# Softmax of the global branch in one scaling pass, with two query blocks side by side and one transpose for their meta columns

## The chip, the cores and the metric

The kernel runs on one core of a Trainium2 chip. A core has five engines that work side by side: TensorE (PE in the profile, its weight loads PEld) for matrix products and transposes, VectorE (DVE), ScalarE (ACT), GpSimd (POOL), and SyncE (SP), which issues most DMAs here. The metric is the device time of one execution in microseconds; a kernel's time is the median of its runs. Work happens in SBUF (128 partitions) and in PSUM, eight banks of 128 x 512 floats, into which TensorE writes. All data are float32; a product takes its operands as two parts each, "hi" (rounded for TensorE) and "lo" (the rest), so that one product is three matmuls.

## What is computed

The reference is two layers of an encoder over 512 grid tokens (64 x 8) and 16 learned meta tokens, 528 in all. Each layer normalises the stream, makes one wide projection and runs two branches side by side, whose gated outputs are merged and added to the stream. The change is in the first, the global branch:

```
def attend(qb):                                   # 8 query heads share 2 key/value heads
    s = einsum('bqkgd,bskd->bkgqs', qb, k) * HEAD_DIM ** -0.5
    p = softmax(s, axis=-1)
    return einsum('bkgqs,bskd->bqkgd', p, v)
```

Queries come in blocks of 128, every one against all 528 keys; the 16 meta queries form a block of their own. The second branch is a windowed attention, in which each query sees a window of 8 x 16 grid neighbours and the meta keys.

## The kernel before

The dense work is a row of projections (`product`, L277): each takes 128 output columns, has eight weight tiles, and for every span of tokens does 24 matmuls (L286 to L288) into a bank of the pool `pp`, which has two. Weights come by DMA into `raw`, ScalarE casts them (L216), GpSimd subtracts (L217). The first layer computes all 528 tokens in two spans of 264 ("full"); the second needs only the 512 grid tokens for most projections and does one span of 512.

Attention is woven between the projections by a clock of the kernel's own: after each span, and in the second layer also in the middle of one, `tick` (L273) is called. Two lists (`Side`, L247) hold the units of the windowed and of the global branch; a unit starts every four ticks, and its steps fall due at ticks after its start as the tables at L35 to L42 say. Within one tick the windowed list comes first. The tile framework then puts each engine's instructions into one fixed order, mostly that of the program; what is traced under `high_priority` goes ahead, and `issue_after(ins)` keeps an instruction behind `ins` in its engine's queue.

A unit of the global branch (`global_unit`, L712) is one head and two blocks of 128 queries; there are 16 in each layer, and two units for meta queries in the first. Its steps:

- `softmax` (L697) for each block: four matmuls (L499, L500) write the scores of 128 queries against 528 keys into the tile `S`, two banks, of which there is only one (it serves the windowed branch's scores `Sb` too). VectorE takes the negated maximum (L704), multiplies it by the query's scale (L705, the per-query norm factor, or 0.125), ScalarE takes the exponential straight from PSUM with that scale and bias and sums it (L706), VectorE inverts the sum (L708) and multiplies (L709).
- `transposes` (L722): the 512 grid columns of both blocks, four 128 x 128 transposes to a bank of the pool `tp`, which has two; then `split` (L170) into hi and lo.
- `meta_transposes` (L734): the last 32 columns of each block, 16 grid and 16 meta keys, transposed one block at a time into the tile `ptm`, and split by `split_down` (L688) into the tile `ga`.
- `sums` (L742): nine matmuls (L746) with the values, and `unit_done` (L770), which puts the two halves of the result together (`combine`, L672) and, after a head pair, applies the gate.

Keys: after their projection `rotated` (L423) applies the rotary positions in a tile of tag E; the norm factors are spread by `pair_factors` (L562), two copies on VectorE ahead of the transposes at L601 and L604, and `keys_scaled` (L598) multiplies them in and calls `stack_soon` (L481), which makes the hi and lo key tiles of both key heads: three ScalarE copies, three VectorE subtractions, two DMAs. `scaled` (L630) and `values` (L636) do the values likewise; the meta tile of the values has rows 0 to 15 cleared. In the windowed branch, `sums` (L876) puts its result together at once (L887, L891).

Buffers in SBUF go by tag (L107); those with tag M hold the input, the stacked queries, the exponentials P and the gated results, 16 single tiles.

Of the kernel before, what the change touches and what calls it, by code (L numbers as in the profile page):

```python
# [18 lines left out]
P = 128  # L19
# [72 lines left out]
def trunk_kernel(ctx: ExitStack, tc: tile.TileContext, xT, w, gn, gf, bias, rope, out):  # L92
# [13 lines left out]

    BUFS = {"h": 16, "M": 16, "O": 8, "K": 4, "T": 2, "R": 2, "B": 9, "E": 6, "G": 8, "KB": 4, "KR": 2, "raw": 3, "whi": 4, "wlo": 4}  # L107

    def slot(tag, name, dt=F32):
        return slots.tile([P, NKEY if tag in ("KB", "KR") else NTOK], dt, tag=tag, bufs=BUFS[tag], name=name)  # L110

# [6 lines left out]

    zero = cpool.tile([P, P], F32, name="zero")
    nc.vector.memset(zero, 0.0)  # L120
# [150 lines left out]
    side_na, side_gqa = Side(NA_AT_TICK), Side(GQA_AT_TICK)  # L271

    def tick():  # L273
# [88 lines left out]
    def feature(k):  # L362
        xs.append(slot("M", f"x0_{k}"))
        nc.sync.dma_start(xs[k], xT[k])
        h.append(normed(0, k, xs[k], NTOK))
        done[0] = h_last["hi"].ins
# [35 lines left out]
    for l in range(DEPTH):  # L402
# [14 lines left out]
        def sum_squares(j, n, qh, ql):  # L417
            for i, (a, b) in enumerate(((0, HALF), (HALF, n))):
                for v in (qh, ql):
                    nc.tensor.matmul(mps[:10, i, :b - a], sel_h[j], v[:, a:b], start=j == 0 and v is qh,  # L420
                                     stop=j == 4 and v is ql, skip_group_check=True)

        def rotated(c, g, full, name):  # L423

            n, j = NTOK if full else NREAL, c - QA
            q, sq = slot("E", f"{name}{l}_{c}"), slot("G", f"{name}s{l}_{c}")
            qh, ql = slot("G", f"{name}h{l}_{c}", F32R), slot("G", f"{name}l{l}_{c}", F32R)
# [20 lines left out]

        def halves_of(tag, name, x, n, eng):

            hi = slot(tag, name, F32R)
# [8 lines left out]
        def stack_q(tag, name, q, n, eng):  # L460

            hi, lo = halves_of(tag, name + "b", q, n, eng)
            first = slot(tag, name + "a", F32R)
            move(first, up, hi, up, n)
            move(first, down, lo, up, n)
            move(hi, up, lo, down, n)
            return first, hi

        def stack_k(tag, name, k, n, eng):

            both = []
            for i, t in enumerate(halves_of(tag, name + "h0", k, n, eng)):
# [8 lines left out]
        def stack_soon(tag, name, k, n):  # L481

            pairs = []
            for hh, r in enumerate((up, down)):
                kh, kl = slot(tag, f"{name}h{hh}", F32R), slot(tag, f"{name}l{hh}", F32R)
# [76 lines left out]
        def pair_factors(t, c, n, name):  # L562

            f = slot("G", f"pf{name}{l}") if n > 1 else tiny.tile([P, P], F32, tag="pf", bufs=1, name=f"pf{name}{l}")
            f = f[:, :P * n].rearrange("p (n h d) -> p n h d", n=n, h=2)
            nc.vector.tensor_copy(f, st["r3"][:, t, c].rearrange("p t (n h) -> p (t n) h", h=2).unsqueeze(3)
                                  .to_broadcast([P, n, 2, HD]))
# [30 lines left out]
        def keys_scaled():  # L598
# [29 lines left out]


        def scaled(tag, c, name, full):  # L630
            t = slot(tag, name)
            for ps, a, b in project(c, full):
                evac["v"] = nc.vector.tensor_mul(t[:, a:b], ps, rbc[:, a:b])
            return t

        def values(v, out, tiles, name):  # L636
# [7 lines left out]
            split(out[:n, u:u + e, :, 0], out[:n, u:u + e, :, 1], src)  # L644
            if n == 32:
                for p in (slice(0, 16), slice(64, P)):
# [4 lines left out]
        v = scaled("E", VA, f"va{l}", True)  # L651
# [4 lines left out]
        side_gqa.later(NORM_AT[l]["values"][1], lambda v=v, VA2=VA2: values(v, VA2, [(4, NTOK - 32, 32)], f"am{l}"))  # L656

# [14 lines left out]
        def combine(tag, o, hh, av, c0, n):  # L672
# [3 lines left out]
            nc.scalar.copy(t[r, :n], av[q, :n])  # L676
            nc.vector.tensor_add(o[r, c0:c0 + n], av[r, :n], t[r, :n])

        def gated(tag, o, gate, name):
            hi, lo = slot(tag, name + "h", F32R), slot(tag, name + "l", F32R)  # L680
# [7 lines left out]
        def split_down(t, tp, rows, a, b):  # L688

            with tc.high_priority():  # L690
                nc.scalar.copy(t[:rows, a:b], tp)
                nc.vector.tensor_sub(t[rows:2 * rows, a:b], tp, t[:rows, a:b].bitcast(F32))


        zgate, oa, o_t, newest = {}, [None] * 4, {}, {}

        def softmax(q, qs, kv, n, scale, name):  # L697
# [4 lines left out]
            p = slot("M", f"P{name}")  # L702
            with tc.high_priority():
                newest["max"] = nc.vector.tensor_reduce(st[:n, 0:1], S[:n, :, :HALF], axis=AX.XY, op=ALU.max, negate=True)  # L704
                nc.vector.tensor_scalar_mul(st[:n, 1:2], st[:n, 0:1], scale)  # L705
                nc.scalar.activation(p[:n].rearrange("p (i k) -> p i k", i=2), S[:n, :, :HALF], AF.Exp,  # L706
                                     bias=st[:n, 1:2], scale=scale, accum_out=st[:n, 2:3])
            nc.vector.reciprocal(st[:n, 3:4], st[:n, 2:3])  # L708
            nc.vector.tensor_scalar_mul(p[:n], p[:n], st[:n, 3:4])  # L709
            return p  # L710

        def global_unit(kv, parts, n, name, done):  # L712

            width = n * len(parts)
            per = min(4, 512 // width)
            c = {"p": [], "t": []}

            def scores(i):
                q, qs, scale = parts[i]
                c["p"].append(softmax(q, qs, kv, n, scale, f"{name}_{i}"))  # L720

            def transposes(kt):  # L722
                tp = bank(ps_t, f"pt{name}_{kt}", "tp")
                for i in range(per):
                    for t, p in enumerate(c["p"]):
                        o = width * i + n * t
                        transposed(tp[:, o:o + n], p[:n, P * (kt + i):P * (kt + i + 1)], n)
                th, tl = slot("G", f"pth{name}_{kt}", F32R), slot("G", f"ptl{name}_{kt}", F32R)
# [49 lines left out]
        def start_meta(kv):  # L778
            for j in (2 * kv, 2 * kv + 1):
                if j not in o_t:  # L780
                    o_t[j] = slot("T", f"oa{l}_{j}")
            return global_unit(kv, [(Q2m[kv], slice(0, 64), 0.125)], 64, f"m{l}_{kv}", lambda av: meta_done(kv, av))

# [14 lines left out]
        def windowed_head(hd):  # L798
# [77 lines left out]
            def sums():  # L876
# [7 lines left out]
                for i, (u, t, c0, a, b) in enumerate(seq):  # L884
                    nc.tensor.matmul(av[:, a:b], rows2(VB2[:, u, hh]), t[:, c0:c0 + b - a], start=i == 0,  # L885
                                     stop=i == len(seq) - 1, skip_group_check=True)
                combine("B", o, hh, av, 0, NREAL)  # L887
                if full:
                    av = bank(ps_t, f"avbm{nm}", "tp")
                    nc.tensor.matmul(av[:, :NMETA], rows2(VB2[:, 0, hh]), c["mt"], start=True, stop=True)  # L890
                    combine("B", o, hh, av[:, :NMETA], NREAL, NMETA)  # L891
                if hh == 1:
                    ob[j] = gated("M", o, zb[j], f"ob{l}_{j}")

# [68 lines left out]
        for m in range(8 + LAG):  # L963
            if m < 8:
                gates[m] = merge_gate(GB, m)
            if m == LAG - 1:
                side_na.finish()
            if m >= LAG:
                mb.append(slot("B", f"mb{l}_{m - LAG}"))
# [3 lines left out]
        for m in range(8 + LAG):  # L973
# [9 lines left out]
            if m >= LAG:  # L983
                ma = slot("G", f"ma{l}_{m - LAG}")
                hi, lo = slot("M", f"mxh{l}_{m}", F32R), slot("M", f"mxl{l}_{m}", F32R)
                end = m == 7 + LAG
# [126 lines left out]
```

## Time and profile before

| | us |
|---|---|
| median of 3 runs | 878.3 (878.14 to 878.75) |
| the profiled execution | 877.75 |
| its span | 876.0 |
| busy TensorE / weight loads | 858.6 / 791.1 |
| busy VectorE / ScalarE / GpSimd | 556.8 / 462.3 / 364.0 |
| granted TensorE clock, mean | 0.997 |

The profile is one execution. Its span goes from the first to the last instruction of the program; the time of the execution has a little around it. A busy share is time in which at least one instruction of the engine ran; matmuls overlap, so TensorE's busy time does not show how fast they followed each other. In the views, L704 is line 704 of the kernel, `P<-S,st` names tiles (output, then inputs, without buffer numbers), and the arrow in "idle before, releaser" says whose end let the instruction start. A wait for several things is put down to the one that came last by the profile.

### The profile page before, as it was taken

What the parts mean: (1) busy time and instruction counts of PE and PEld (TensorE: products, weight loads), DVE (VectorE), ACT (ScalarE), POOL (GpSimd) and SP (SyncE); (2) the same over time, 40 slices, a digit from 0 to 9 for tenths busy, and PEclk for the clock granted to TensorE, in tenths of its full rate; (3) what the DMA queues carried; (4) which work ended last, traced back from release to release, by engine and by line L of the source; (5) the groups of instructions that cost most, each with busy time, mean ns of one, the idle gap of its engine ahead of it and who ended that gap; (6) DMA issues with size and microseconds to landing.
All of it is one profiled execution on the core that took longest, in us unless ns stands there. A gap on an engine that the chain in (4) does not pass through costs nothing.

```text
span 876.0 us, 16169 instructions
## 1 busy us (share of the span) xinstructions
PE 858.6 (98%) x5984; PEld 791.1 (90%) x5984; DVE 556.8 (64%) x1264; ACT 462.3 (53%) x1027; POOL 364.0 (42%) x298
## 2 busy tenths in 40 slices
PE   9999999999999999999999999999999999999996
PEld 8999999999999999999998989888888888888785
DVE  6985678676774674436447757688867746544632
ACT  8644666565764554334345446566656645443422
POOL 5564343343233333454764643334332233334640
PEclk9999999999999999999999999999999999999998
DMA  8364444334222221324655654234432222222602
GB/s 278 109 161 123 112 120 118 89 110 122 73 71 74 73 74 61 109 86 143 168 129 128 158 160 129 79 109 133 124 109 73 76 81 73 85 84 97 205 24 97
DMA packets 67232, 96.90 MB, mean 111 GB/s; under 512 B 23376, under 2 KB 23888, under 8 KB 67152
## 3 DMA queue, kind: packets, MB, share of 16 engines
q1 hardware_dynamic: 66432, 94.79, 37.6%
q8 instruction: 47, 0.77, 0.4%
q10 hardware_dynamic: 720, 1.06, 0.3%
q14 instruction: 33, 0.27, 0.1%
HBM read 76.72 MB, written 4.19 MB: 92 GB/s over the span
## 4 chain that ended last, share of the span: by engine, by line
PE 83%; DVE 8%; ACT 5%; issue 2%; DMA 2%; POOL 0%; SPq 0%; POOLq 0%; ACTq 0%; DVEq 0%
PE pp L286 17%; PE pp L288 17%; PE pp L287 17%; PE y L288 3%; PE y L286 3%; PE y L287 3%; PE av L746 3%; PE pt L116 3%; PE avb L885 2%; PE S L500 2%; PE pf L1046 2%; PE pf L1048 2%; PE S L499 2%; PE pf L1047 1%; DVE Pb L827 1%
## 5 line engine op out<-in xcount | busy, mean ns | idle before, releaser
L217 POOL TENSOR_TENSOR wlo<-raw,whi 128x512 fp32r<-128x512 f32 x214 | 286.7, 1344 | 431.0 <-ACT whi L216 385.2
L286 PE MATMUL pp<-hh,whi 128*128 128x264 f32 (+1 forms) x1056 | 334.8, 317 | 1.8 <-DVE qb L943 1.0
L288 PE MATMUL pp<-hh,wlo 128*128 128x264 f32 (+1 forms) x1056 | 329.3, 312 | 0.0
L287 PE MATMUL pp<-hl,whi 128*128 128x264 f32 (+1 forms) x1056 | 328.2, 311 | 0.0
L216 ACT CAST whi<-raw 128x512 fp32r<-128x512 f32 x214 | 131.2, 620 | 157.6 <-PE pp L287 61.9
L286 PEld LDWEIGHTS pp<-hh,whi 128*128 128x128 f32 x1056 | 198.6, 188 | 12.0 <-DVE qb L943 1.2
L288 PEld LDWEIGHTS pp<-hh,wlo 128*128 128x128 f32 x1056 | 198.9, 188 | 10.8
L287 PEld LDWEIGHTS pp<-hl,whi 128*128 128x128 f32 x1056 | 199.3, 189 | 9.0
L706 ACT ACTIVATE P<-S,st,r 128x528 f32<-128x528 f32 x64 | 50.6, 790 | 52.7 <-DVE st L705 45.3
L953 DVE TENSOR_TENSOR mg<-pp,rbc 128x264 f32<-128x264 f32 (+1 forms) x48 | 24.8, 517 | 45.3 <-PE pp L288 44.5
L704 DVE TENSOR_REDUCE st<-S 128x1 f32<-128x528 f32 x64 | 45.0, 703 | 13.0 <-PE S L500 12.2
L173 DVE TENSOR_TENSOR ptl<-pt,pth 128x512 fp32r<-128x512 f32 x64 | 43.9, 687 | 13.1 <-ACT pth L172 12.6
L172 ACT CAST pth<-pt 128x512 fp32r<-128x512 f32 x64 | 37.3, 584 | 10.3 <-PE pt L116 9.3
L116 PE MATMUL pt<-ident,P 128*128 128x128 f32 x256 | 39.7, 274 | 2.0 <-DVE st L705 1.0
L708 DVE RECIPROCAL st<-st 128x1 f32<-128x1 f32 x64 | 10.5, 164 | 45.5 <-ACT P L706 45.1
L823 ACT ACTIVATE Pb<-Pb,stb 128x208 f32<-128x208 f32 (+1 forms) x64 | 31.0, 485 | 12.5 <-DVE stb L821 12.4
L287 PE MATMUL pp<-mxl,whi 128*128 128x264 f32 x128 | 36.5, 285 | 0.0
L286 PE MATMUL pp<-mxh,whi 128*128 128x264 f32 x128 | 36.5, 285 | 0.0
L288 PE MATMUL pp<-mxh,wlo 128*128 128x264 f32 x128 | 36.4, 284 | 0.0
L709 DVE TENSOR_SCALAR P<-P,st 128x528 f32<-128x528 f32 x64 | 34.7, 542 | 2.2
L954 ACT ACTIVATE mg<-mg 128x264 f32<-128x264 f32 (+1 forms) x48 | 23.7, 493 | 23.0 <-DVE mg L953 22.8
L746 PE MATMUL av<-pth,VA 128*128 128x256 f32 x128 | 35.1, 296 | 0.0
(611 smaller groups left out, 1765.7 us busy)
## 6 DMA issues: line engine op xcount, KB each, us to landing
raw<-in_w_dram SPq DMA_DIRECT2D x214, 256.0 KB, 2.7
bias<-in_bias_dram SPq DMA_DIRECT2D x16, 480.0 KB, 4.0
rawl<-in_w_dram SPq DMA_DIRECT2D x16, 256.0 KB, 3.1
x<-in_xT_dram SPq DMA_DIRECT2D x8, 264.0 KB, 4.6
xr<-in_xT_dram SPq DMA_DIRECT2D x8, 264.0 KB, 3.9
x1d<-xt SPq DMA_DIRECT2D x32, 64.0 KB, 2.8
xf<-x1d SPq DMA_DIRECT2D x8, 256.0 KB, 4.9
KB_0l<-kb SPq DMA_DIRECT2D x8, 140.0 KB, 2.6
```

The source lines that it names most:

```text
L116: nc.tensor.transpose(ps, src, ident[:n, :n])
L172: split_at["hi"] = nc.scalar.copy(hi, src)
L173: split_at["any"] = nc.vector.tensor_sub(lo, src, hi.bitcast(F32))
L216: cast = nc.scalar.copy(hi, raw)
L217: sub = nc.gpsimd.tensor_sub(lo, raw, hi.bitcast(F32))
L286: nc.tensor.matmul(ps, wh, rh[:, a:b], start=i == 0, stop=False)
L287: nc.tensor.matmul(ps, wh, rl[:, a:b], start=False, stop=False)
L288: nc.tensor.matmul(ps, wl, rh[:, a:b], start=False, stop=i == n - 1)
L704: newest["max"] = nc.vector.tensor_reduce(st[:n, 0:1], S[:n, :, :HALF], axis=AX.XY, op=ALU.max, negate=True)
L706: nc.scalar.activation(p[:n].rearrange("p (i k) -> p i k", i=2), S[:n, :, :HALF], AF.Exp, bias=st[:n, 1:2], scale=scale, accum_out=st[:n, ...
L709: nc.vector.tensor_scalar_mul(p[:n], p[:n], st[:n, 3:4])
L746: nc.tensor.matmul(c["av"], rows2(c["t"][i][0]), c["t"][i][1], start=i == 0, stop=i == 8)
```

## The change

Six edits belong together.

- The scores are multiplied by the query's scale and their maximum is taken in one VectorE pass that writes them to SBUF; ScalarE negates the maximum and takes the exponential in place, from SBUF, with scale 1.
- The two blocks' P lie side by side in one tile of 2 x 528 columns. The first block has its meta keys last and the second first, so that the four meta stretches of 16 columns meet in the middle, and one transpose of 64 columns serves both. For this the keys get a copy of their 16 meta columns in front (528 + 16), and the block chooses its stretch of 528. The meta tile of the values is laid out to match (64 rows).
- Tag M holds 8 pairs in place of 16 tiles. Keys move to a buffer of tag KR, values to one of tag `bias`.
- The key head 1 half of `stack_soon` comes four ticks later, and the two factor copies go to ScalarE.
- In the windowed branch, putting the sums together is deferred to the end of the tick.
- The additions of `combine` are kept behind the newest maximum in VectorE's queue.

```
-    BUFS = {"h": 16, "M": 16, ...
+    BUFS = {"h": 16, "M": 8, ...
...
+    def two(tag, name, dt=F32):
+        if tag == "M":
+            t = slots.tile([P, 2, NTOK], dt, tag=tag, bufs=BUFS[tag], name=name)
+            return t[:, 0], t[:, 1]
+        return slot(tag, name + "a", dt), slot(tag, name + "b", dt)
...
+    eighth = cpool.tile([P, 1], F32, name="eighth")
+    nc.vector.memset(eighth, 0.125)
...
     def tick():
         side_na.tick()
         side_gqa.tick()
+        while ending:
+            ending.pop(0)()
...
-            nc.vector.tensor_copy(f, st["r3"][:, t, c].rearrange("p t (n h) -> p (t n) h", h=2).unsqueeze(3)
+            nc.scalar.copy(f, st["r3"][:, t, c].rearrange("p t (n h) -> p (t n) h", h=2).unsqueeze(3)
                                   .to_broadcast([P, n, 2, HD]))
...
-            KA2.extend(stack_soon("K", f"KA{l}", k, NTOK))
+            both_ends = keys[0]
+            nc.vector.tensor_copy(both_ends[:, :NMETA], k[:, NREAL:])
+            KA2.extend(stack_soon("K", f"KA{l}", both_ends, NTOK + NMETA, 0))
+            side_gqa.later(4, lambda: KA2.extend(stack_soon("K", f"KA{l}", both_ends, NTOK + NMETA, 1)))
...
-            nc.vector.tensor_add(o[r, c0:c0 + n], av[r, :n], t[r, :n])
+            with ExitStack() as held:
+                if "max" in newest:
+                    held.enter_context(tc.issue_after(newest["max"].ins))
+                nc.vector.tensor_add(o[r, c0:c0 + n], av[r, :n], t[r, :n])
...
+        def split_meta(parts):
+            with tc.high_priority():
+                for g, (to, tp) in enumerate(parts):
+                    nc.scalar.copy(to[32 * g:32 * g + 32], tp[32 * g:32 * g + 32])
+                for g, (to, tp) in enumerate(parts):
+                    nc.vector.tensor_sub(to[64 + 32 * g:96 + 32 * g], tp[32 * g:32 * g + 32], to[32 * g:32 * g + 32].bitcast(F32))
...
-                score(S[:n, i, :HALF], q, KA2[kv], qs, slice(HALF * i, HALF * (i + 1)))
+                score(S[:n, i, :HALF], q, KA2[kv], qs, slice(k0 + HALF * i, k0 + HALF * (i + 1)))
...
-                newest["max"] = nc.vector.tensor_reduce(st[:n, 0:1], S[:n, :, :HALF], axis=AX.XY, op=ALU.max, negate=True)
-                nc.vector.tensor_scalar_mul(st[:n, 1:2], st[:n, 0:1], scale)
-                nc.scalar.activation(p[:n].rearrange("p (i k) -> p i k", i=2), S[:n, :, :HALF], AF.Exp,
-                                     bias=st[:n, 1:2], scale=scale, accum_out=st[:n, 2:3])
+                newest["max"] = nc.vector.tensor_tensor_reduce(
+                    p[:n].rearrange("p (i k) -> p i k", i=2), S[:n, :, :HALF], scale[:n].unsqueeze(2).to_broadcast([n, 2, HALF]),
+                    1.0, -3e38, ALU.mult, ALU.max, st[:n, 0:1])
+                nc.scalar.mul(st[:n, 1:2], st[:n, 0:1], -1.0)
+                nc.scalar.activation(p[:n], p[:n], AF.Exp, bias=st[:n, 1:2], scale=1.0, accum_out=st[:n, 2:3])
...
+            first_token = (0, NMETA)
...
-                c["p"].append(softmax(q, qs, kv, n, scale, f"{name}_{i}"))
+                if i == 0:
+                    c["both"] = slots.tile([P, 2 * NTOK], F32, tag="M", bufs=BUFS["M"], name=f"P{name}")
+                    c["p"] = [c["both"][:, NTOK * t:NTOK * (t + 1)] for t in range(len(parts))]
+                softmax(c["p"][i], q, qs, kv, NMETA - first_token[i], n, scale, f"{name}_{i}")
...
-                for t, p in enumerate(c["p"]):
-                    transposed(tp[:32, n * t:n * t + n], p[:n, NTOK - 32:NTOK], n)
+                rows = 32 * len(parts)
+                transposed(tp[:rows, :n], c["both"][:n, NTOK - 32:NTOK - 32 + rows], n)
                 tm = pad_tile("ga")
-                split_down(tm, tp[:32, :width], 32, 0, width)
+                split_meta([(tm[:, n * t:n * (t + 1)], tp[:, :n]) for t in range(len(parts))])
...
-                combine("B", o, hh, av, 0, NREAL)
+                def collect(av=av):
+                    combine("B", o, hh, av, 0, NREAL)
+                    if full:
+                        combine("B", o, hh, c["avm"], NREAL, NMETA)
+                    if hh == 1:
+                        ob[j] = gated("M", o, zb[j], f"ob{l}_{j}")
...
+                ending.append(collect)
```

More of the change, by code (lines that the diff above doesn't have):

```diff
@@ L102, in trunk_kernel @@
     ps_a = ctx.enter_context(tc.tile_pool(name="ps_a", bufs=1, space=PS))
-    BUFS = {"h": 16, "M": 16, "O": 8, "K": 4, "T": 2, "R": 2, "B": 9, "E": 6, "G": 8, "KB": 4, "KR": 2, "raw": 3, "whi": 4, "wlo": 4}
+    BUFS = {"h": 16, "M": 8, "O": 8, "K": 4, "T": 2, "R": 2, "B": 9, "E": 6, "G": 8, "KB": 4, "KR": 2, "raw": 3, "whi": 4, "wlo": 4}
     def slot(tag, name, dt=F32):
-        return slots.tile([P, NKEY if tag in ("KB", "KR") else NTOK], dt, tag=tag, bufs=BUFS[tag], name=name)
+        n = NKEY if tag in ("KB", "KR") else NTOK + NMETA if tag == "K" else NTOK
+        return slots.tile([P, n], dt, tag=tag, bufs=BUFS[tag], name=name)
+    def two(tag, name, dt=F32):
[3 more added lines that the diff above has]
+        return slot(tag, name + "a", dt), slot(tag, name + "b", dt)
     def bank(pool, name, tag):
@@ L116, in transposed @@
         nc.tensor.transpose(ps, src, ident[:n, :n])
-    zero = cpool.tile([P, P], F32, name="zero")
+    zero = slot("T", "zero")[:, :P]
     nc.vector.memset(zero, 0.0)
@@ L362, in feature @@
     def feature(k):
-        xs.append(slot("M", f"x0_{k}"))
+        if k % 2 == 0:
+            xs.extend(two("M", f"x0_{k}"))
         nc.sync.dma_start(xs[k], xT[k])
@@ L460, in stack_q @@
         def stack_q(tag, name, q, n, eng):
-            hi, lo = halves_of(tag, name + "b", q, n, eng)
-            first = slot(tag, name + "a", F32R)
+            first, hi = two(tag, name, F32R)
+            hi, lo = halves_of(hi, q, n, eng)
             move(first, up, hi, up, n)
@@ L471, in stack_k @@
             both = []
-            for i, t in enumerate(halves_of(tag, name + "h0", k, n, eng)):
+            for i, t in enumerate(halves_of(slot(tag, name + "h0", F32R), k, n, eng)):
                 pair = [slot(tag, f"{name}{'hl'[i]}{hh}", F32R) if hh or i else t for hh in range(2)]
@@ L479, in stack_k, with stack_soon @@
             return list(zip(*both))
-        def stack_soon(tag, name, k, n):
+        def stack_soon(tag, name, k, n, hh):
             pairs = []
-            for hh, r in enumerate((up, down)):
+            for hh, r in ((hh, (up, down)[hh]),):
                 kh, kl = slot(tag, f"{name}h{hh}", F32R), slot(tag, f"{name}l{hh}", F32R)
@@ L630, in scaled @@
         def scaled(tag, c, name, full):
-            t = slot(tag, name)
+            t = slot(tag, name) if tag != "bias" else slots.tile([P, 960], F32, tag=tag, bufs=2, name=name)
             for ps, a, b in project(c, full):
                 evac["v"] = nc.vector.tensor_mul(t[:, a:b], ps, rbc[:, a:b])
+            if tag == "bias":
+                nc.vector.tensor_mul(t[:, NTOK:NTOK + NMETA], ps[:, b - a - NMETA:b - a], rbc[:, NREAL:NTOK])
+                nc.gpsimd.memset(t[:, NTOK + NMETA:NTOK + 2 * NMETA], 0.0)
             return t
@@ L644, in values @@
             split(out[:n, u:u + e, :, 0], out[:n, u:u + e, :, 1], src)
-            if n == 32:
-                for p in (slice(0, 16), slice(64, P)):
+            if n == 32 or e == 1 and n == 64:
+                for p in (slice(0, 16), slice(64, P))[:1 + (n == 32)]:
                     nc.gpsimd.memset(out[p, u].rearrange("p h s d -> p (h s d)").bitcast(F32), 0.0)
@@ L886, in sums @@
                                      stop=i == len(seq) - 1, skip_group_check=True)
-                combine("B", o, hh, av, 0, NREAL)
-                if full:
[L889 to L893, printed above, removed]
+                def collect(av=av):
[4 more added lines that the diff above has]
+                        ob[j] = gated("M", o, zb[j], f"ob{l}_{j}")
+                if full:
+                    c["avm"] = bank(ps_t, f"avbm{nm}", "tp")[:, :NMETA]
+                    nc.tensor.matmul(c["avm"], rows2(VB2[:, 0, hh]), c["mt"], start=True, stop=True)
+                ending.append(collect)
             return prepare, scores, transposes1, transposes2, transposes3, sums
```

32 lines of the change are left out of this document (18 added, 14 removed).

## The prediction

> **What bounds the kernel now.** I read the page's head first, then what TensorE waited for, then the order of time around single waits.
>
> ```profile
> span 876.0 us, 16169 instructions
> ...
> PE 858.6 (98%) x5984; PEld 791.1 (90%) x5984; DVE 556.8 (64%) x1264; ACT 462.3 (53%) x1027; POOL 364.0 (42%) x298
> ```
>
> TensorE (PE) is busy for 98% of the span, its weight loads for 90%; VectorE (DVE) and ScalarE (ACT) for two thirds and a half. So only two things can move the end: TensorE work that goes, and moments in which TensorE stands still. Work on VectorE or ScalarE counts only where it makes one of those. What TensorE waited for (us in total, times, longest):
>
> ```profile
> PE vtd L641 <- DVE na L692: 1.4, 3, 0.8
> PE Sb L499 <- ACT P L706: 1.4, 4, 0.7
> ...
> PE pt L116 <- DVE st L705: 1.0, 1, 1.0
> PE pp L286 <- DVE qb L943: 1.0, 1, 1.0
> ...
> PE pt L116 <- DVE P L709: 0.9, 2, 0.6
> PE pp L286 <- DVE rh L178: 0.5, 1, 0.5
> ...
> PE S L500 <- DVE KA0l L490: 0.4, 1, 0.4
> ```
>
> These seven rows make 6.6 us; each names an instruction that the change touches or one queued near it. The pool of waits is under one per cent of the span, so no reordering can win more than that.
>
> **The change, part by part.**
>
> *One transpose for the meta columns.* Every unit of two query blocks now issues two `ptm` transposes; the change issues one with 64 rows out. First a row of the tile's own view (least, median and greatest ns), then the order of time (start us, length us):
>
> ```profile
> L116 PE MATMUL ptm<-ident,P x64: 270/272/285, 80.2 to 774.7; 128*32 128x128 f32 x64
> 80.15 0.38 PE L116 MATMUL ptm<-ident,P 128*32 128x128 f32 x2
> 80.29 0.37 PE L286 MATMUL pp<-hh,whi 128*128 128x264 f32 x1
> 80.49 0.28 PE L287 MATMUL pp<-hl,whi 128*128 128x264 f32 x1
> 80.62 0.28 PE L288 MATMUL pp<-hh,wlo 128*128 128x264 f32 x1
> ```
>
> 64 of them are 32 pairs. TensorE overlaps matmuls, so their price is the distance of starts, not the 0.272 us. From the first `ptm` (80.15) to the second `pp` (80.49) pass 0.34 us; one `pp` step is 0.13 us (80.49 to 80.62); 0.21 us is left for two transposes, about 0.105 us each. Saved: 32 x 0.105 = 3.4 us. Bounds: if most of the 0.21 us is a cost of changing over from transposes to matmuls, which one transpose pays as well, only some 0.03 us goes with the second one (1.0 us in all); if what goes is the whole 0.14 us between first `ptm` and first `pp`, 4.5 us. I take 3.4, the even split.
>
> The Trainium skill, TensorE: Matmul & The Clock Gate, Part 4: PE-mode transpose, gives about 275 ns for a transpose inside a kernel and says that access latency dominates it. The row's duration (272 ns) agrees, its distance of starts does not; what the sum would be by that price stands with the rivals.
>
> *Softmax: maximum, scale, exponential.* Now a maximum straight from PSUM, a 128x1 multiply on VectorE, and an exponential that reads PSUM with a per-row scale. The score tile has one buffer, so the next scores (also the windowed branch's) wait for the exponential. After: one VectorE pass multiplies, writes to SBUF and keeps the maximum, a 128x1 negation on ScalarE, and an exponential from SBUF with a constant scale. The same kind of pass stands in the windowed branch (L821, L823). The groups (count | busy us, mean ns | idle before), and one row of the meta units' tile:
>
> ```profile
> L704 DVE TENSOR_REDUCE st<-S 128x1 f32<-128x528 f32 x64 | 45.0, 703 | 13.0 <-PE S L500 12.2
> L705 DVE TENSOR_SCALAR st<-st,r 128x1 f32<-128x1 f32 x64 | 13.2, 206 | 0.9
> L706 ACT ACTIVATE P<-S,st,r 128x528 f32<-128x528 f32 x64 | 50.6, 790 | 52.7 <-DVE st L705 45.3 <-DVE ob L677 4.4 <-PE y L288 1.4
> L821 DVE CUSTOM_DVE_ANT_0 Pb<-Sb,bias 128x272 f32<-128x272 f32 x32 | 12.8, 436 | 0.0
> L821 DVE CUSTOM_DVE_ANT_0 Pb<-Sb,bias 128x208 f32<-128x208 f32 x32 | 11.9, 372 | 6.0 <-PE Sb L500 3.9 <-PE sm L500 2.0
> L821 DVE DVE_READ_ACCUMULATOR2_ANT stb<- 128x1 f32 x64 | 5.3, 83 | 0.0
> L823 ACT ACTIVATE Pb<-Pb,stb 128x272 f32<-128x272 f32 x32 | 16.3, 509 | 0.0
> L823 ACT ACTIVATE Pb<-Pb,stb 128x208 f32<-128x208 f32 x32 | 14.7, 461 | 12.5 <-DVE stb L821 12.4
> L706 ACT ACTIVATE Pm<-Sm,stm x2: 696/698/699, 95.5 to 264.1; 64x528 f32<-64x528 f32 x2
> L836 ACT ACTIVATE pm<-sm,smt 16x16 f32<-16x16 f32 x8 | 2.0, 249 | 0.0
> L676 ACT COPY cmb<-avbm 64x16 f32<-64x16 f32 x8 | 1.3, 166 | 0.1
> ```
>
> The pass: 64 ns more for 64 columns (372 to 436), so 528 columns cost 436 + 256 = 692 ns, and 83 ns for reading the maximum: 0.775 us, against 703 + 206 = 0.909 us now. The exponential: from SBUF 48 ns for 64 columns, so 509 + 192 = 701 ns; the meta units' one with a constant scale took 698 ns; so 0.70 us against 0.79 now, between 0.70 and 0.79 in the range. The negation is not in the trace: the nearest ScalarE rows are 166 ns (64x16 copy) and 249 ns (16x16 with a per-row operand); I take 0.19, near the copy, since it has constants alone. Chain from scores to exponentials: now 0.703 + 0.206 + 0.790 = 1.70 us; after 0.775 + 0.19 + 0.70 = 1.67 us (1.64 to 1.81 by the bounds). So the chain to the transposes stays as long as it was. Price on the path: nothing; what changes is that the score tile is free after the first 0.775 us. The wait of `Sb` for the exponential (1.4 us) goes. VectorE also no longer lets other work in between the maximum and its multiply, as here:
>
> ```profile
> 84.00 0.71 DVE L704 TENSOR_REDUCE st<-S 128x1 f32<-128x528 f32 x1
> 84.63 1.37 DVE L669 SCALAR_TENSOR_TENSOR za<-za_0t,za 128x528 f32<-128x528 f32 x1
> 85.92 0.20 DVE L705 TENSOR_SCALAR st<-st,r 128x1 f32<-128x1 f32 x1
> ```
>
> A gate's 1.37 us held the exponential back. ScalarE can let a weight cast in instead, so I count nothing for it.
>
> The Trainium skill, ScalarE: Activation LUTs, What ACT_TABLE_LOAD costs, prices an ACTIVATE with constant scale and bias at 186 ns and 0.833 ns per element, an estimate of 187 ns for the negation; no run here shows that size. With it the sum would be the same.
>
> *Meta split.* One copy and one subtraction of 32x256 become two each of 32x128.
>
> ```profile
> L692 DVE TENSOR_TENSOR ga<-ptm,ga 32x256 fp32r<-32x256 f32 x32 | 13.3, 414 | 5.1 <-ACT ga L691 4.3
> 504.73 0.27 DVE L173 TENSOR_TENSOR VA<-vtam,VA 32x128 fp32r<-32x128 f32 x1
> ```
>
> VectorE: 32 x (2 x 0.27 - 0.414) = 4.0 us more, against 64 x 0.134 = 8.6 us less above; ScalarE gets some 12 us of negations, less 6 us of exponentials. Neither engine reaches its limit by that: nothing on the path, if no single queue is late where TensorE needs it.
>
> *Key stacking and factors.* The second half of the keys is split four ticks later, and the factor copies go from VectorE to ScalarE.
>
> ```profile
> 53.66 1.51 DVE L566 COPY pfk<-rh 128x512 f32<-128x512 f32 x1 [0.69 <-POOL rh L183]
> 55.09 1.31 DVE L566 COPY pfkm<-rh 128x128 f32<-128x128 f32 x1
> ...
> 499.69 4.40 DVE L490 TENSOR_TENSOR KA1l<-k,KA1h 64x528 fp32r<-64x528 f32 x3 [0.79 <-ACT KA1h L489]
> ...
> 504.12 0.69 DVE L943 SCALAR_TENSOR_TENSOR qb<-pp,rbc 128x512 f32<-128x512 f32 x1
> ```
>
> Three subtractions of 4.40 us together stand ahead of `qb`, whose projection bank TensorE waits for: one third is deferred, and the wait (1.0 us) goes. In the first layer 2.8 us of copies leave VectorE ahead of the keys: the waits on `rh` (0.5) and `KA0l` (0.4) go. The 16 extra key columns add one small copy. The deferred part, its two DMAs on SP's queue too, is needed by heads 4 to 7 only, some ten units later; it can meet another evacuation, at worst for the same 1.0 us again.
>
> *Windowed sums put together later, additions behind the newest maximum.* This aims at one place:
>
> ```profile
> 131.64 0.69 DVE L677 TENSOR_TENSOR ob<-avb,cmb 64x512 f32<-64x512 f32 x1 [0.73 <-ACT cmb L676]
> 132.37 0.71 DVE L704 TENSOR_REDUCE st<-S 128x1 f32<-128x528 f32 x1
> 133.11 0.56 DVE L173 TENSOR_TENSOR VB<-vtb,VB 128x384 fp32r<-128x384 f32 x1
> 133.81 0.41 PE L116 MATMUL pt<-ident,P 128*128 128x128 f32 x2 [1.02 <-DVE st L705]
> ```
>
> The view blames L705, but `pt` starts 0.14 us after the `VB` subtraction ends, which frees one of two transpose banks. With `ob` (0.69) moved behind the maximum, `VB` ends some 0.7 us earlier: of 1.0 us, 0.7 go. What is queued behind a held addition: the gate product and the next split, which nobody on TensorE needs at once. But the meta sum `avbm` now keeps the other transpose bank through that tick.
>
> Pairs of tiles in place of single ones (tag M), keys and values in other slots: no instruction; what hides them is that an older unit is finished before its buffer is taken again. If not, a unit's pass waits; zero to 1 us.
>
> **Sum.** 3.4 (transposes) + 1.4 (`Sb`) + 1.0 (`qb`) + 0.5 + 0.4 (keys) + 0.7 (`pt`) = 7.4 us. Of the 4.0 us of waits I give 1.0 back for new ones: 6.4 us. The profiled execution took 877.75 us, 1.75 more than its span, so 871.35 by its measure; the median of the runs, 878.3, lies 0.55 higher: 871.9 us.
>
> **Rivals.** (1) Waits only move: another late VectorE operation, like `na` before `vtd` (1.4 us), comes up in place of each; the transposes alone remain, 878.3 - 3.4 = 874.9. For it: VectorE's rows in the second layer stay nearly as full. (2) The transposes are mostly change-over cost (1.0 us) and waits only move: 877.3, no change. (3) Slower: the chain of each unit becomes longer than the place that the compiled order of TensorE gives `pt`. At units where normalised P (L709) is just in time, each 0.1 us more is a stall of 0.1 us. The upper bounds, 0.249 for the negation and 0.79 for an exponential from SBUF, make 1.81 us, and another 0.1 us if ScalarE hands its own result on slowly (the nearest: 0.14 us from the end of `VB` to `pt`): 0.2 us over now, on 32 units 6.4 us. Against it 3.4 and 1.4 us: the kernel is 1.6 us slower, 879.9. It decides from a lengthening of 0.15 us per unit (4.8 / 32). Against it: 701 and 698 ns for the nearest exponentials. (4) A transpose stands on the path with its whole duration: 32 x 0.272 = 8.7 us, and 3.0 of waits: 866.6. Against it: the distances of starts above. That is what the skill's page would give.
>
> **How the numbers follow.** Forecast 0.50, (1) 0.22, (2) 0.10, (3) 0.13, (4) 0.05. About 0.2% (1.8 us) is what a measurement of this kernel can tell from no change. Faster: forecast, (1) and (4), 0.77; same: (2), 0.10; slower: (3), 0.13. The range runs from 867.0, near (4), past (2) with 1.0 us of new waits in it, to 878.5; it leaves out (3) and part of (4). The forecast's own range is 869 to 874 by the bounds 1.0 to 4.5 and the waits.
>
> **What would show it.** `ptm` transposes with 32 instead of 64 entries and a shorter step from them to the next `pp`; no `Sb` wait for ScalarE; the pass near 0.69 us, the exponential near 0.70, the negation under 0.25; no wait for `qb` near 505 us; ScalarE up by some 10 us. I am wrong if `pt` waits for normalised P in many units, or `vtd` and `tb` wait more than now.

## The result and the profile after

The changed kernel takes 873.07 us (median of 4 runs, 872.49 to 873.59), the kernel before 878.52 us beside it; the ratio is 0.9935, 95% interval 0.9918 to 0.9952. It is faster by 5.4 us, 0.6%. Three runs of later versions, two of one and one of another, took far longer than the rest, and their medians are given without them.

The head of the page after the change:

```profile
span 871.1 us, 16225 instructions
...
PE 854.4 (98%) x5952; PEld 788.6 (91%) x5952; DVE 548.6 (63%) x1296; ACT 481.3 (55%) x1130; POOL 363.2 (42%) x298
```

TensorE has 32 matmuls fewer and is as full as before; VectorE lost 8 us of work, ScalarE gained 19 us. The new groups (count | busy us, mean ns | idle before; L745 is the pass, L748 the negation, L749 the exponential, L731 and L733 the split of the meta columns):

```profile
L749 ACT ACTIVATE P<-P,st 128x528 f32<-128x528 f32 x64 | 47.2, 737 | 1.8
L745 DVE CUSTOM_DVE_ANT_1 P<-S,r 128x528 f32<-128x528 f32 x64 | 45.1, 705 | 13.9 <-PE S L521 12.6
L733 DVE TENSOR_TENSOR ga<-ptm,ga 32x128 fp32r<-32x128 f32 x64 | 18.2, 285 | 7.8 <-ACT ga L731 6.6
L731 ACT CAST ga<-ptm 32x128 fp32r<-32x128 f32 x64 | 16.2, 254 | 6.5 <-PE ptm L124 6.0
L748 ACT ACTIVATE st<-st 128x1 f32<-128x1 f32 x64 | 13.0, 202 | 30.6 <-DVE st L745 29.8
L745 DVE DVE_READ_ACCUMULATOR2_ANT st<- 128x1 f32 x64 | 5.3, 83 | 0.0
```

What TensorE waited for, all of the rows:

```profile
PE vtd L671 <- DVE na L725: 1.9, 4, 0.7
PE vtc L671 <- DVE ptl L183: 1.4, 1, 1.4
PE warm L132 <- DVE one L138: 1.0, 1, 1.0
PE S L521 <- DVE KA0l L511: 0.9, 1, 0.9
PE tc L124 <- DVE tal L183: 0.8, 1, 0.8
PE pp L415 <- DVE hl L316: 0.7, 2, 0.5
PE tb L124 <- DVE tal L183: 0.6, 2, 0.4
PE pp L301 <- ACT qs L453: 0.5, 1, 0.5
PE pt L124 <- DVE VB L183: 0.4, 1, 0.4
PE tb L124 <- DVE ptl L183: 0.3, 1, 0.3
PE av L792 <- DVE ga L733: 0.2, 1, 0.2
PE ta L124 <- DVE Pb L873: 0.2, 1, 0.2
```

Of the seven waits that the prediction listed, those of `Sb`, of `qb`, of `rh` and of normalised P have gone, and 0.4 us of the bank's wait at `pt` is left. But `vtd`, `vtc`, `tc` and `tb` wait for VectorE's subtractions (`na`, `ptl`, `tal`), 5.0 us in all where it was 2.7, and `S` waits 0.9 us for the keys, where it was 0.4. Around the one transpose, in order of time:

```profile
80.03 0.27 PE L124 MATMUL ptm<-ident,P 128*64 128x128 f32 x1
80.05 0.37 PE L301 MATMUL pp<-hh,whi 128*128 128x264 f32 x1
80.26 0.28 PE L302 MATMUL pp<-hl,whi 128*128 128x264 f32 x1
```

From `ptm` to the second `pp` pass 0.23 us; before, with two transposes, it was 0.34 us. Lining up the start of the same projection matmul in the two traces shows where the gain lies: 3.0 us at the end of the first layer's attention, 4.9 us at the last projection.

### The profile page after: what moved, and what is told of

It is laid out like the page before. It is cut to its first block, busy times and chain, and to the rows that moved or that the text cites. A ratio compares the mean times of both kernels' runs of the same rounds, so it can differ in the third digit from the quotient of the medians.

```text
span 871.1 us, 16225 instructions
## 1 busy us (share of the span) xinstructions
PE 854.4 (98%) x5952; PEld 788.6 (91%) x5952; DVE 548.6 (63%) x1296; ACT 481.3 (55%) x1130; POOL 363.2 (42%) x298
## 4 chain that ended last, share of the span: by engine, by line
PE 85%; DVE 7%; ACT 4%; issue 1%; DMA 1%; SPq 0%; POOL 0%; POOLq 0%; DVEq 0%; ACTq 0%
PE pp L303 18%; PE pp L301 18%; PE pp L302 18%; PE y L303 3%; PE y L301 3%; PE y L302 3%; PE av L792 3%; PE pt L124 3%; PE avb L931 2%; PE S L521 2%; PE S L520 2%; PE pf L1098 2%; PE pf L1100 2%; DVE Pb L873 1%; PE pf L1099 1%
## 5 line engine op out<-in xcount | busy, mean ns | idle before, releaser
L745 DVE CUSTOM_DVE_ANT_1 P<-S,r 128x528 f32<-128x528 f32 x64 | 45.1, 705 | 13.9 <-PE S L521 12.6
L183 DVE TENSOR_TENSOR ptl<-pt,pth 128x512 fp32r<-128x512 f32 x64 | 44.0, 689 | 14.6 <-ACT pth L182 13.7
L749 ACT ACTIVATE P<-P,st 128x528 f32<-128x528 f32 x64 | 47.2, 737 | 1.8
L869 ACT ACTIVATE Pb<-Pb,stb 128x208 f32<-128x208 f32 (+1 forms) x64 | 31.1, 486 | 16.2 <-DVE stb L867 15.9
L302 PE MATMUL pp<-mx,whi 128*128 128x264 f32 x128 | 36.6, 286 | 0.0
L301 PE MATMUL pp<-mx,whi 128*128 128x264 f32 x128 | 36.4, 285 | 0.0
L303 PE MATMUL pp<-mx,wlo 128*128 128x264 f32 x128 | 36.3, 283 | 0.0
L751 DVE TENSOR_SCALAR P<-P,st 128x528 f32<-128x528 f32 x64 | 32.0, 500 | 2.1
L792 PE MATMUL av<-ptl,VA 128*128 128x256 f32 x128 | 33.0, 280 | 0.0
```

The costliest lines, as they stand in the source:

```text
L183: split_at["any"] = nc.vector.tensor_sub(lo, src, hi.bitcast(F32))
L301: nc.tensor.matmul(ps, wh, rh[:, a:b], start=i == 0, stop=False)
L302: nc.tensor.matmul(ps, wh, rl[:, a:b], start=False, stop=False)
L303: nc.tensor.matmul(ps, wl, rh[:, a:b], start=False, stop=i == n - 1)
L745: newest["max"] = nc.vector.tensor_tensor_reduce(p[:n].rearrange("p (i k) -> p i k", i=2), S[:n, :, :HALF], scale[:n].unsqueeze(2).to_broa ...
L749: nc.scalar.activation(p[:n], p[:n], AF.Exp, bias=st[:n, 1:2], scale=1.0, accum_out=st[:n, 2:3])
```

## The experiments

All are edits of the changed kernel, timed beside the kernel before; that one's medians were 878.4 to 879.2 us. Differences between versions below are differences of their medians, and versions of different batches can shift against each other by as much: counted against the kernel before of the same batch, the 2.8, 5.7, 6.3 and 3.0 us below are 2.1, 5.1, 5.7 and 2.4.

**Only the layout and the one transpose.** Softmax, key stacking, factor copies and sums as before.

```
-                newest["max"] = nc.vector.tensor_tensor_reduce(...)
-                nc.scalar.mul(st[:n, 1:2], st[:n, 0:1], -1.0)
-                nc.scalar.activation(p[:n], p[:n], AF.Exp, ...)
+                newest["max"] = nc.vector.tensor_reduce(st[:n, 0:1], S[:n, :, :HALF], ...)
+                nc.vector.tensor_scalar_mul(st[:n, 1:2], st[:n, 0:1], factor)
+                nc.scalar.activation(p[:n]..., S[:n, :, :HALF], AF.Exp, bias=st[:n, 1:2], scale=factor, ...)
...
+            KA2.extend(stack_soon(..., 1));  nc.vector.tensor_copy(f, ...);  collect()
```

> Of the change only the layout: two blocks side by side, meta keys at both ends, one transpose for the meta columns; the softmax, the key stacking, the factor copies and the putting together of sums are as before. Theory A (the forecast: transposes at 0.105 us and waits that go because of the other edits): 878.5 - 3.4 = 875.1, so ratio 0.996 to before. Rival B (waits only move, transposes are the whole gain): the same as the changed kernel, about 873 to 874. Rival C (a transpose counts with its whole 0.272 us): 869.8.

881.96 us, ratio 1.0035 (1.0023 to 1.0048): slower than the kernel before. All three expectations miss. Something in the layout or the split of the meta columns costs more than the transposes save.

**The transpose twice.**

```
+                if len(parts) == 2:
+                    transposed(tp[:rows, :n], c["both"][:n, NTOK - 32:NTOK - 32 + rows], n)
```

> The changed kernel with its one transpose for the meta columns issued twice in each of the 32 units of two blocks (the second writes the same values again). If a transpose costs its distance of starts, 0.108 us: 3.5 us more than the changed kernel, about 876.5. Rival: cost of changing over, 0.03 us each: 874. Rival C, the whole duration: 881.8.

875.83 us, ratio 0.9963 (0.9951 to 0.9976): 2.8 us more than the changed kernel, 0.09 us for each of 32 (0.07 by the 2.1 us). The price by the distance of starts holds nearly; 0.03 and 0.27 us do not. In the trace the two transposes of a pair start 0.109 us apart (median of the 32), as the two of a pair did before the change.

**The old softmax.** The first edit of the first experiment alone.

> The changed kernel with the softmax of before (maximum from the score tile, multiply on the vector engine, exponential from the score tile with the query's scale). Theory A: the wait of the windowed scores for the exponential comes back (1.4 us), about 874.5 with rows of that wait in the profile. Rival B (waits move): within 0.5 us of the changed kernel, 873. A second rival, that the new pass makes the chain to the transposes shorter where the vector engine let other work in between: 875 to 876.

879.38 us, ratio 1.0004 (0.9995 to 1.0012): 6.3 us more than the changed kernel, so the softmax edit alone makes up for more than the whole gain. All three expectations miss. What TensorE waited for, and ScalarE:

```profile
PE Sb L520 <- ACT P L748: 2.8, 5, 1.3
...
PE S L520 <- ACT P L748: 1.2, 3, 0.7
...
PE pt L124 <- DVE P L751: 1.0, 2, 0.7
```

```profile
ACT P L748 <- DVE st L747: 51.5, 46, 2.2
```

These waits of matmuls for the held score tile are 4.0 us, and ScalarE waits 51.5 us in all for maximum and multiply; in the changed kernel its row at L748 says 29.8.

**The old placements.** Both halves of the keys at once, factor copies on VectorE, sums at once, additions free.

> The changed kernel with four placements undone: second half of the keys split at once, factor copies on the vector engine, windowed sums put together at once, additions not held behind the newest maximum. Theory A: the waits of the projection for qb (1.0), rh (0.5) and of pt (0.7) come back: about 875.3. Rival B (other waits go in turn): within 0.7 us of the changed kernel, 872.4 to 873.8.

876.09 us, ratio 0.9967 (0.9955 to 0.9979): 3.0 us more than the changed kernel. But of the waits named, `qb` and `rh` stay away, and `pt` for `VB` goes from 0.4 to 0.9 us; the rest is `vtd` (2.7) and `tc` (1.5) and the keys' own (`S` for `KA0h`, 1.4). The sum is near Theory A's, the places are not: lined up, 2.0 us are lost before 100 us, and 0.8 us in the second layer.

**Two transposes, one split.** The old meta columns in the new layout.

```
-                transposed(tp[:rows, :n], c["both"][:n, NTOK - 32:NTOK - 32 + rows], n)
+                for t in range(len(parts)):
+                    o = NTOK - 32 + NMETA * t
+                    transposed(tp[:32, n * t:n * t + n], c["both"][:n, o:o + 32], n)
-                split_meta(...)
+                split_down(tm, tp[:32, :width], 32, 0, width)
```

> The changed kernel with two transposes of 32 columns for the meta columns of a unit and one copy and one subtraction of 32x256, as before; everything else stays. If the one transpose is worth its 0.108 us in each of 32 units and the doubled copies and subtractions are hidden: about 876.6. If the doubled copies and subtractions (0.156 us more on the vector engine in each unit, 0.154 us on the scalar engine) cost waits, part of it comes back: 873 to 875.5; if they cost more than the transposes save: under 873.

870.14 us, ratio 0.9903 (0.9888 to 0.9918): under 873, the third case. With the one transpose undone, the kernel is 2.9 us faster than the changed one. Its waits and its split:

```profile
PE vtd L671 <- DVE na L725: 0.7, 3, 0.3
PE vtc L671 <- DVE ptl L183: 0.5, 1, 0.5
...
PE tb L124 <- DVE ptl L183: 0.3, 1, 0.3
```

```profile
L725 DVE TENSOR_TENSOR ga<-ptm,ga 32x256 fp32r<-32x256 f32 x32 | 13.3, 414 | 6.4 <-ACT ga L724 5.7
```

No `tc` row is left, and `vtd`, `vtc` and `tb` make 1.5 us. Against the kernel that also has two transposes but split copies (875.83), the transposes of 32 rows with one copy and one subtraction, in place of those of 64 rows with two of each, are worth 5.7 us.

**Only the layout**, with the old meta columns, softmax and placements.

> Of the change only the layout without its purpose: two blocks side by side, meta keys at both ends, buffers in pairs, but two transposes of 32 columns and one copy and one subtraction for the meta columns, and the softmax, key stacking, factor copies and sums of before. Theory F (the layout costs nothing, the doubled copies and subtractions cost about 5.7 us and the one transpose saves 2.8): some 2.9 us under the layout with the one transpose (881.96), that is 879, as before. Theory H (the layout's own buffers and longer keys cost): 880 to 882.

Ratio 1.0007 (0.9998 to 1.0015), 878.98 us: as before, theory F. Pairs of buffers and longer keys cost nothing that can be measured, and the first experiment's loss comes with the one transpose of 64 rows and its doubled copies.

**The score tile held.** The pass and the negation stay, the exponential reads PSUM.

```
-                nc.scalar.activation(p[:n], p[:n], AF.Exp, bias=st[:n, 1:2], scale=1.0, ...)
+                nc.scalar.activation(p[:n]..., S[:n, :, :HALF], AF.Exp, bias=st[:n, 1:2], scale=scale[:n], ...)
```

> The changed kernel, in which the exponential reads the score tile with the query's scale instead of the scaled copy: the vector engine's pass, the negation and the order stay, but the score tile is held until the exponential has read it. Theory D (the softmax edit gains by freeing the score tile after the pass): close to the kernel with the old softmax, 878 to 879.4, with waits of S and Sb for the scalar engine in the profile. Theory E (it gains because nothing comes between maximum and exponential, or because the vector engine is relieved): close to the changed kernel, 873 to 874.5.

874.78 us, ratio 0.9958 (0.9945 to 0.9970):

```profile
PE S L520 <- ACT P L749: 1.4, 2, 1.1
PE Sb L520 <- ACT P L749: 1.2, 1, 1.2
```

The waits for the tile are back (2.6 us), but the time is only 1.7 us longer, and the exponential too is longer here (0.792 us from PSUM with the query's scale, 0.737 from SBUF). So of the 6.3 us, at most 1.7 come from freeing the tile, and some 4.6 from the rest of the softmax edit: nearer to theory E, though just above its range. Counting in the traces from the start of a maximum to the start of its exponential: 1.56 us on average before, 1.11 us after, 1.12 us here, and 35 of 64 over 1.5 us before, 9 after. Before the change, other work of VectorE stood between the maximum and its multiply for 0.36 us on average, and for more than 0.1 us in 42 of 64.

**Keys at once**, and **sums at once**, each alone.

> The changed kernel with both halves of the keys split at once. Forecast: the wait of a projection for qb (1.0 us) comes back, 874.1. Of the 3.0 us that the four placements together are worth, this would be a third. Rival: the wait does not come back, since the factor copies have left the vector engine: 873.1.

874.10 us, ratio 0.9948 (0.9936 to 0.9961). The time is the forecast's, the place is not: there is no wait for `qb`. Lined up, the 1.2 us by which the span is longer are lost in the first layer, where P is late once (0.9 us). The intervals of both ratios overlap, so the size stays uncertain.

> The changed kernel with the windowed sums put together at once and the additions not held behind the newest maximum. Forecast: 0.7 us of the transposes' wait for VB come back: 873.8. Rival: the additions ahead of the maximum delay the softmax in many units: 874.5 to 876. Second rival: nothing, 873.1.

874.83 us, ratio 0.9957 (0.9945 to 0.9970): 1.8 us, nearest the first rival. `pt` for `VB` waits 0.5 us more, and `vtd` (2.8) and `tc` (2.2) wait more too; lined up, half of the loss falls in the second layer, after 600 us, where nothing had been forecast. With the four placements at 3.0, little is left for the factor copies, which were not tried alone.

**Windowed multiplications on ScalarE**, in the second layer.

```
-                    nc.vector.tensor_scalar_mul(pb[b], pb[b], st[:, 2, b:b + 1])
+                    (nc.vector.tensor_scalar_mul if full else nc.scalar.mul)(pb[b], pb[b], st[:, 2, b:b + 1])
```

> The changed kernel; in the second layer the four multiplications of the windowed branch's exponentials by the inverse sum are on the scalar engine. They take 0.35 us each alone and up to 1.46 us on the vector engine beside GpSimd's work, and hold 16.6 of the 130 us from 560 to 690. Theory G (the changed kernel's waits in the second layer come from a vector queue that these stretched multiplications make late): waits of vtd, vtc, tc and tb shrink, 869.5 to 871. Rival: the scalar engine gets late in its place: 873 to 876.

871.46 us, ratio 0.9921 (0.9909 to 0.9934): 1.6 us less than the changed kernel, just above the range that theory G gave. `tc` no longer waits, `vtc` 0.5; `vtd` still waits, 2.3.

**One transpose and one split.** The 64 rows are copied and subtracted once, and each block has its own values.

```
+                    nc.scalar.copy(tm[:rows, :n], tp[:rows, :n])
+                    nc.vector.tensor_sub(tm[64:64 + rows, :n], tp[:rows, :n], tm[:rows, :n].bitcast(F32))
...
+                    for t in range(len(parts)):
+                        nc.tensor.matmul(c["av"][:, n * t:n * (t + 1)], rows2(VA2[:, 4 + t, kv]), c["m"][:, :n], ...)
```

> The changed kernel with one transpose and also one copy and one subtraction, of 64x128, for the meta columns of a unit; the two blocks then take a matmul of 128 columns each with their own values, in place of one of 256. If the doubled copies and subtractions are what costs: vector engine 0.29 us in a unit in place of 0.57, so under the kernel with two transposes (870.1): the transposes' 2.8 less the second matmul's some 1.7 gives 868.5 to 870. If instead the one transpose itself costs (its 64 rows come later): 873.

871.82 us, ratio 0.9925 (0.9912 to 0.9938): between the two cases, and not the best version. From the first matmul with the meta values to the next instruction pass 0.172 us where it was 0.120 with one matmul (medians of 32), so 0.057 of the transpose's 0.109 us are left; and `vtd` still waits 1.9 us, once 1.3. If the doubled copies alone cost the 5.7 us, this version would have come out near 869.1 (873.07 - 5.7 + 32 x 0.052). It is 2.7 us above that, so either the one transpose of 64 rows has a part in the cost, or the edit's own additions do: it moves a small buffer of the norm factors and adds a second copy of the meta values. These were not tried apart.

**The same with the windowed multiplications on ScalarE.**

> The former kernel with the windowed multiplications of the second layer on the scalar engine too. Theory G with a vector queue that is in time again: little more to win, 868 to 869.5, less than the same move wins in the changed kernel. Rival (scalar engine late): 870 to 872.

870.39 us, ratio 0.9910 (0.9896 to 0.9924): the move is worth some 1.5 us here as well; the time lies in the rival's range. The gain is as much as in the changed kernel and not less, so theory G is not what makes the two kernels differ.

The fastest version is the one with two transposes and one split (870.14); the last one is not to be told apart from it.

## Why the prediction was right, and where it was wrong

The forecast was 871.9 us, the result 873.07. Direction and size hold, but two of its steps do not: one was missing some 5.7 us of cost, the other some 4.9 us of gain. They nearly cancel, so that the total came out 1.2 us from the forecast is in good part luck.

*The transposes.* Forecast 0.105 us each, 3.4 us; the trace gives 0.34 - 0.23 = 0.11 us, issuing them again costs 2.8 us (2.1 in its batch). Right, or a little too high. Rival (4), the whole duration, is out, and with it the price that the Trainium skill (TensorE: Matmul & The Clock Gate, Part 4: PE-mode transpose) would set: the duration of 272 ns stands in both traces, and the next matmul starts long before it ends.

*The meta split.* "Nothing on the path, if no single queue is late where TensorE needs it": this step failed. The work was sized well (0.285 us a piece against 0.27), but the way of splitting with 0.156 us more of VectorE and 0.154 us more of ScalarE in each unit cost 5.7 us, twice what the transpose saves. The sum of ScalarE's work also left out these copies, 4.9 us in all (16.2 - 11.3); it rose by 19 us, not by some 10. The cost lies in the second layer, between 560 and 690 us: lined up, the two versions with two transposes (875.83 and 870.14) part by 4.4 us there. There the changed kernel waits 4.3 us for `vtc`, `tc`, `tb` and `vtd`, the one with a single split 1.1. VectorE is busy for 63% of the span, but for 101.3 of these 130 us, 78%, and so the share over the span hid that it is behind in this stretch. After the change, in order of time:

```profile
588.41 2.67 DVE L873 TENSOR_SCALAR Pb<-Pb,stb 128x272 f32<-128x272 f32 x2
...
590.99 0.68 DVE L710 TENSOR_TENSOR ob<-avb,cmb 64x512 f32<-64x512 f32 x1
...
595.37 0.69 DVE L183 TENSOR_TENSOR tal<-ta,tah 128x512 fp32r<-128x512 f32 x1
...
596.21 0.60 PE L124 MATMUL tc<-ident,Pb 128*32 128x128 f32 x4 [0.76 <-DVE tal L183]
```

Two multiplications take 2.67 us and all behind them comes late, to the subtraction `tal` that frees a bank for `tc`. In the kernel with a single split the same pair is nearly as long, and `tc` does not wait:

```profile
587.58 2.32 DVE L874 TENSOR_SCALAR Pb<-Pb,stb 128x272 f32<-128x272 f32 x2
...
594.20 0.69 DVE L183 TENSOR_TENSOR tal<-ta,tah 128x512 fp32r<-128x512 f32 x1
...
595.77 0.60 PE L124 MATMUL tc<-ident,Pb 128*32 128x128 f32 x4
```

Of the 1.17 us by which `tal` comes later after the change, 0.35 us are the pair's. VectorE began the pair 0.83 us later already, while the projections on TensorE ran 0.48 us earlier. The group of these multiplications from 560 to 690 us, in the changed kernel and in the one with a single split:

```profile
L873 DVE TENSOR_SCALAR Pb<-Pb,stb 128x208 f32<-128x208 f32 (+1 forms) x24 | 16.6, 736 | 0.1
```

```profile
L874 DVE TENSOR_SCALAR Pb<-Pb,stb 128x208 f32<-128x208 f32 (+1 forms) x24 | 13.7, 610 | 0.2
```

The same 24 instructions take 2.9 us more: 11 of them are over 0.5 us long in place of 8, and each of the long ones lies beside an instruction of GpSimd. But they took 14.0 us before the change, and moving them to ScalarE wins the same with one split as with two, so they hardly explain the difference. How the 5.7 us divide between them, the pieces' own time and the transpose of 64 rows is open: with single copies and one transpose the group also takes 13.7 us, and the kernel is still 1.7 us slower than the best.

*Softmax.* "Price on the path: nothing", and 1.4 us for the freed tile: the mechanism of the tile was right (at most 1.7 us), the rest was mis-sized. The instructions come out near the forecast (0.705 + 0.083, 0.202 and 0.737 us against 0.692 + 0.083, 0.19 and 0.70), so the bare chain is no shorter. What I saw and then wrote "so I count nothing for it", other VectorE work between the maximum and its multiply, was there in 42 of 64 softmaxes: with the wait for the tile the edit is worth 6.3 us in place of 1.4, and the way from the start of the maximum to the end of the exponential is shorter by 0.5 us on average (2.35 before, 1.85 after). Whether the some 4.6 us beside the tile come from the closed gap or from 7.7 us less work on VectorE (64 x (0.703 + 0.206 - 0.705 - 0.083)) was not tried apart. The negation took 202 ns; the estimate of 187 from the Trainium skill (ScalarE: Activation LUTs, What ACT_TABLE_LOAD costs) was near.

*Placements.* Forecast 2.6 us less 1.0 for new waits; measured 3.0. The waits for `qb` and `rh` went, but neither came back when the placements alone were undone, so the sum fits and the places do not: lined up, 2.4 us were won in the first layer, 2.0 of them before 100 us, and 0.8 us in the second. That the sum fits is luck in part.

*The rivals.* (1), that the waits only move, is near the view (10.0 us of waits before, 8.9 after, over all rows), but the experiments show two large effects of opposite sign below that. (2) is out. The condition of (3), a chain longer by 0.15 us, did not arise: its four pieces add up to 1.73 us against 1.70, and no `pt` waits for normalised P any more. Of the prediction's two signs of being wrong, the second did arise: `vtd` waits 1.9 us where it was 1.4, and `tb` 0.9 where it was 0.3. It pointed at the late stretch.

*The cap on waits.* That "no reordering can win more than that", under one per cent of the span, failed too: between the kernel before and the version with one split, which issue the same number of matmuls, lie 8.4 us, but the rows of matmuls' waits fall only from 10.0 to 4.6. The weight loads' own waits show the rest. The score tile's row among them was, before:

```profile
PEld Sb L499 <- ACT P L706: 3.5, 8, 1.1
```

The prediction counted 1.4 us, from the row of the matmuls. All waits of weight loads add up to some 21 us before, 20 after, 27 with the old softmax and 13 with two transposes and one split. The span less these waits is 850 to 851.5 us in each of the eight traced versions with 5952 matmuls, and 854 to 856 us in each of the five with 5984.

In all: layout 0.5, transposes -2.8, the split with 64 rows +5.7, softmax -6.3, placements -3.0, which adds to -5.9, against -5.4 measured; each term is open by some 0.7 us, as far as batches shift. Softmax and placements together are worth 8.9 us with the doubled copies (881.96 - 873.07) and 8.8 without (878.98 - 870.14), so they do not hang on them.

## What to carry to other kernels

Where one engine is full, an instruction saved on it is worth its distance of starts, and an instruction added on another engine is free only if that engine is in time in the stretch at hand; read its share by stage, not over the span, and read the waits of weight loads beside those of matmuls. A short dependent instruction on a busy in-order queue costs what slips in ahead of it, so a pass that folds it in can be worth more than its duration. And a change of several edits that comes out as forecast may hold one that loses: undoing them one at a time found a faster kernel.

## What the runs showed of the hardware

- A multiplication by a per-row factor from SBUF to SBUF on VectorE (L873) takes 0.35 us in the median and up to 1.46 us, four times as long; after the change each of the 13 over 0.5 us lies beside an instruction of GpSimd for at least 0.89 of its time. The Trainium skill (GPSIMD Engine Reference, Specifications) says that GpSimd shares its SBUF interfaces with VectorE and contends with its instructions in a 2-port mode or with two SBUF inputs. The trace agrees in that VectorE is slow beside GpSimd; which mode the multiplication runs in, no trace here shows.
- The exponential of 528 columns from SBUF with a constant scale takes 0.737 us, more than the 0.698 us of 64 rows from PSUM and the 0.701 us drawn from shorter rows.
- A transpose to 64 rows is no longer than one to 32 (274 and 272 ns on average), and the second of a pair starts 0.109 us after the first with either.
